# Operands, splits and halos tied to other places of the order in the input projection of a hybrid encoder block

## The chip, the cores and the metric

The kernel runs on one core of a Trainium2 chip. The time is that of one execution on the device, in microseconds (us). A core has a matrix engine (PE, TensorE), three engines for elementwise work (DVE, or VectorE; ACT, or ScalarE; POOL, or GpSimd) and SP (SyncE), which issues this kernel's DMAs. Each engine takes its instructions strictly in its own order, and semaphores tie the engines to each other. The profile records one execution.

## The reference

The input x has 2048 tokens of 1024 values. One projection makes 9232 columns of it, from which two mixers and two merging gates are fed:

```python
h = rms_norm(x, norm_pre_g)
proj = einsum('bsd,de->bse', h, w_in)              # 1024 -> 9232
u_a, z_a, q, k, v, o, z_b, gates, g_a, g_b = split(proj)
pooled = multiscale_pool(u_a)                      # centred windows of 2, 4, 8, 16 tokens, minus the token
y_a = (group_linear(pooled, pool_mix_w) * pool_scale) * silu(z_a)
q, k = silu(depthwise_conv5(concat(q, k)))         # 5 taps along the tokens
hb = mlstm(q, k, v, gates, forward) + mlstm(..., backward)   # 4 heads, chunks of 128
y_b = rms_norm_per_head(hb) * mlstm_norm_g * sigmoid(o) * silu(z_b)
merged = sigmoid(g_a + b0) * (y_a @ w_proj_pool) + sigmoid(g_b + b1) * (y_b @ w_proj_mlstm)
return x + rms_norm(merged @ w_out, norm_post_g)
```

All arithmetic is in float32, and the result has to be close to the reference at that precision.

## The kernel before

**Stages.** `phase1` is the projection, in two halves of 1024 tokens; in the profile the first half lasts to about 800 us and the second to about 1490. Behind it come the mLSTM (to about 1830), the two projections with the merge, and the output projection with norm and residual (about 2180 to the end). Only `phase1` is changed.

**Float32 in parts.** A float32 operand is split into an upper part, rounded to the matmul's own type, and a lower part, the remainder: `split` lets ACT write the upper part (L98) and lets DVE or POOL subtract it (L102). A product of two split operands is three matmuls (upper by upper, upper by lower, lower by upper; L110, L111, L112, and L500 to L502 in the plain form).

**Pairs.** Each half works through 36 pairs of 128 columns, numbered from 0. Pairs 0 and 1 (the first columns of g_a and g_b) are multiplied plainly while the operands of the other form are still being built (`quarters`). From pair 2 on `strassen` needs 7 products for the 8 of a 2 by 2 block form. The tokens' side has the blocks A11, A12, A22 and the sums S1 to S4; the weights' side has B11, B21, B22 and T1 to T4. The products are added up in PSUM banks A, B, C (two buffers each); ACT copies bank A to p1 (L463), and DVE reads bank B into u2 and u3 (L469, L474). `read_banks` lists these reads and the outputs of DVE. Half of a pair's products are issued together with the first products of the next one. For pairs of kind q, k, v and u `collect` puts the four blocks of the result into two tiles named raw (L684 on ACT, L685 on DVE).

**The tokens' operands** are made by `operands` in each half. x comes in as eight tiles that lie in places of other pools (`room`): raw, acc, and two in the ring wc of split weights. `sums` squares and adds them, four matmuls with a column of ones (ssqp, L258) sum over the partitions, and rstd is spread over partitions by four matmuls (rbp, L183). `busy` (L281) is a matmul whose result nobody reads; one stands ahead of the ssqp matmuls and one behind rbp. `combos` then builds S1, S2, S3 and S4 with DVE and splits them: the lower parts of S1 and S3 by POOL, those of S2 and S4 by DVE.

**The weights' operands.** In the first half `load` fetches a pair's columns (wraw, L346), `prep_w` takes differences on DVE (wt, L426) and splits them, and `keep_w` stores T1 to T4 to DRAM (L413). In the second half `again_w` loads the kept ones back (L389) and splits only B11, B21 and B22. Pools: wraw 3 tiles, wc 10, wt 3, and raw 3, acc 4, p 6 for the rest.

**Beside the pairs.** At the start of each half `gates` multiplies the 16 gate columns into a PSUM tile of the tag tr (gps; two buffers) and ACT copies it out (gsb, L671). In the first half `fold` multiplies pool_mix_w into w_in's u columns (fps, L373, in the same tag) ahead of the pairs that need it. In the second half, `masked` (L1017 on) adds a mask to tiles nm, which lie in the pool wt, on POOL (L1023), and `split_ahead` loads a piece of w_proj_pool (x, tile wp), splits it (upper part in a second tile wp) and stores both. Both stand behind the pair's last weight load (`self.read`). For pairs q and k a convolution of five taps follows (`conv`; ACT L713, DVE L718, POOL L723), for u the sums over windows (L775), for v transposes by PE (vtr, L744) into tiles vn with a column of ones. The second half needs a few columns of the first, the halos, which DVE copies into raw (L705, L765) with zeros at the far end (L706, L766); L737 and L738 write the ones and zeros of vn.

**What sets the order.** The functions issue instructions in program order; a scheduler then makes one order for each engine, from priorities (`tc.high_priority`) and a model of the costs. `tc.issue_after(ins)` puts each instruction issued in its block, if it is of the engine of `ins`, behind `ins` in that engine's order. It adds no wait for other engines.

The prep of pair 2 in the first half is tied behind one of the scalings of x, that of pair 3 to nothing:

```python
with tc.issue_after(self.scaled[8].ins) if i == 2 else ExitStack():
    self.prep_w(W, load(i), wc, wt)
```

Of the kernel before, what the change touches and what calls it, by code (L numbers as in the profile page):

```python
# [81 lines left out]
class Kernel:  # L82
# [122 lines left out]

    def combos(self, H, j, a11, a12, a21, a22):

        nc = self.nc
        s1, s3, s2, s4 = a22, a21, a11, a12
        nc.vector.tensor_tensor(s1, a21, a22, op=ALU.add)  # L210
        nc.vector.tensor_tensor(s3, a11, a21, op=ALU.subtract)
        nc.vector.tensor_tensor(s2, s1, a11, op=ALU.subtract)
        self.put(H, "S2", j, s2, "act", "dve")
        self.put(H, "S1", j, s1, "act", "pool")
        self.put(H, "S3", j, s3, "act", "pool")
        return lambda: (
            nc.vector.tensor_tensor(s4, a12, s2, op=ALU.subtract),
            self.put(H, "S4", j, s4, "act", "dve"),
        )

    def operands(self, half, H, hp, wc, pool, psum):
# [4 lines left out]
        room = {}  # L226
        for b, q, where in ((0, 0, "raw"), (0, 2, "acc"), (0, 1, "acc"), (0, 3, "acc"), (1, 0, "raw"), (1, 2, "raw"), (1, 1, wc), (1, 3, wc)):
            if where is wc:
                t = wc.tile([P, 2, BLK], F32, tag="wc", name=self.nm("xT"))
            else:  # L230
                t = pool.tile([P, 2, BLK], F32, tag=where, name=self.nm("xT"))
            room[b, q] = t
# [15 lines left out]
        def sums():  # L248
            acc = None
            for kt in range(KT):  # L250
                sq = pool.tile([P, BLK], F32, tag="p", name=self.nm("sq"))
                nc.scalar.activation(sq, X[kt][0], AF.Square)
                if acc is not None:
                    nc.vector.tensor_tensor(sq, sq, acc, op=ALU.add)
                acc = sq
            ps = psum.tile([P, 4], F32, tag="tr", name=self.nm("ssqp"), bufs=2)
            for i in range(4):
                nc.tensor.matmul(ps[:, i : i + 1], acc[:, i * P : (i + 1) * P], self.one_c, start=True, stop=True)  # L258
            busy(X[7][0][:, :P], X[7][0])
            ssq = pool.tile([P, 4], F32, tag="ssq", name=self.nm("ssq"), bufs=2)  # L260
            ends = self.rstd_of(ssq, ps, 0, 0)
            self.rows_of(0, 0, rb[:, :BLK], psum)
            busy(self.rstd[:, :1].to_broadcast([P, P]), X[7][0])
            return ends
# [34 lines left out]
        for b in range(2):  # L299
# [22 lines left out]
            yield  # L322
        ends = [self.combos(H, j, X[j][0], X[4 + j][0], X[j][1], X[4 + j][1]) for j in range(4)]
        yield
# [118 lines left out]
    def strassen(self, H, W, psum, pool, out, n=BLK, swap=False):  # L443
# [18 lines left out]
        p1 = pool.tile([P, n], F32, tag="p", name=self.nm("p1"))  # L462
        nc.scalar.activation(p1, bank["A"], AF.Copy)  # L463
        if self.edge:
# [46 lines left out]
    def phase1(self):  # L511
        tc, nc, a = self.tc, self.nc, self.a
        with ExitStack() as es:
# [25 lines left out]
            for half in range(2):  # L539
# [53 lines left out]
                for i in range(2, n):  # L593
# [7 lines left out]
                    with tc.high_priority(offset=200):  # L601
                        if half == 0:
                            with tc.issue_after(self.scaled[8].ins) if i == 2 else ExitStack():
                                self.prep_w(W, load(i), wc, wt)
                        else:
                            self.again_w(W, i, wr, wc)
# [7 lines left out]
                    if half == 1 and PRE <= i < PRE + 2 * KT:  # L614
                        with tc.issue_after(self.read.ins):
                            self.split_ahead(*divmod(i - PRE, KT))
                    if half == 0:
# [10 lines left out]
                    if half == 0 and i in FOLDS[1:]:  # L628
                        next(fold)
                    next(this)  # L630
                    rest = this
                    if half == 0 and i + 1 in FOLDS:
# [25 lines left out]
    def gates(self, half, H, W, psum, pool):  # L658
        nc = self.nc
        for b in range(2):  # L660
# [9 lines left out]
            g = pool.tile([32, BLK], F32, tag="p", name=self.nm("gsb"))  # L670
            nc.scalar.activation(g, ps, AF.Copy)  # L671
            t0 = half * HALF + b * BLK
# [3 lines left out]
    def collect(self, H, W, psum, pool, width, off):  # L676
# [4 lines left out]
        def out(i, ps, add):  # L681
            d = t[i % 2][:, off + (i // 2) * BLK : off + (i // 2 + 1) * BLK]
            if add is None:
                return nc.scalar.activation(d, ps, AF.Copy)  # L684
            return nc.vector.tensor_tensor(d, ps, add, op=ALU.add)  # L685

# [3 lines left out]
    def pair_qk(self, half, kind, h, H, W, psum, pool):  # L690
# [3 lines left out]
        for i in range(2):  # L694
# [9 lines left out]
            else:  # L704
                nc.vector.tensor_copy(raw[:, 0:4], self.halo_qk[:, ct, :])  # L705
                nc.vector.memset(raw[:, HALF + 4 : HALF + 6], 0.0)  # L706
                self.conv(pool, kind, h, i, raw, HALF + 2, HALF - 2)
# [24 lines left out]
    def pair_v(self, half, kind, h, H, W, psum, pool):  # L732
        nc = self.nc
        t = yield from self.collect(H, W, psum, pool, HALF, 0)
        for b in range(2):
            hi, lo = (pool.tile([P, 4, DH + 2], F32R, tag="acc", name=self.nm(f"vn{p}")) for p in "hl")
            nc.vector.memset(hi[:, :, DH:].bitcast(F32), 1.0)  # L737
            nc.vector.memset(lo[:, :, DH:].bitcast(F32), 0.0)  # L738
            for c2 in range(2):
# [11 lines left out]
    def pair_u(self, half, kind, g, H, W, psum, pool):  # L751
# [6 lines left out]
        for i in range(2):  # L758
# [5 lines left out]
            else:  # L764
                nc.vector.tensor_copy(raw[:, 0:16], self.halo_u[:, ct, :])  # L765
                nc.vector.memset(raw[:, HALF + 16 : HALF + 24], 0.0)  # L766
            s, span, at = raw, 1, 8 - w // 2
# [235 lines left out]

    def split_ahead(self, e, kt):

        nc = self.nc
        x, hi = (self.wt_pool.tile([P, 512], F32, tag="wt", name=self.nm("wp")) for _ in range(2))
        nc.sync.dma_start(x, self.a["w_proj_pool"][:, kt, e * 512 : (e + 1) * 512])
        self.split(hi.bitcast(F32R), x.bitcast(F32R), x, "act", "dve")
        for p, t in enumerate((hi, x)):  # L1010
# [716 lines left out]
```

## Time and profile before

| | us |
|---|---|
| median of 3 runs | 2350.88 |
| lowest and highest | 2348.56 and 2352.04 |
| profiled execution | 2351.66 |
| its span, first to last instruction | 2349.9 |
| its mean granted PE clock, of full speed | 0.994 |
| PE busy | 2291.2 (98%) |
| DVE, POOL, ACT busy | 1428.9, 1182.4, 884.2 |

Timeline rows give the start, the duration, the engine, line and operation, the tiles (out<-in) and shapes, a count where several are put together, and in brackets how long the engine was idle before and what ended that. Rows of waits read "engine tile line <- what ended it: us in total, times, longest". In the rows of stretches each engine has its busy time and the number of its instructions; then come the granted clock, the share of the DMA engines' time and the bytes moved.

### The profile page before, as it was taken

The numbers are of one execution on the slowest core, as the hardware profiler recorded it, in microseconds if no ns is written. First come the engines' busy times: TensorE is split into PE (matmuls) and PEld (weight loads), VectorE is DVE, ScalarE is ACT, GpSimd is POOL, SyncE is SP. The second block draws the span as 40 slices with busy tenths as digits, with TensorE's granted clock in tenths as the row PEclk, the third lists the DMA queues.
The fourth block names the chain that finished last, engine by engine and source line by source line (L and its number), as shares of the span: only waits on it lengthen the run. The fifth ranks groups of instructions, "written<-read, shape, count | busy, mean of one in ns | idle before, by whom it ended". The sixth has DMA issues, their size and how long they took to land.

```text
span 2349.9 us, 32919 instructions
## 1 busy us (share of the span) xinstructions
PE 2291.2 (98%) x11545; PEld 1938.3 (82%) x11545; DVE 1428.9 (61%) x2383; ACT 884.2 (38%) x1795; POOL 1182.4 (50%) x917
## 2 busy tenths in 40 slices
PE   7999999999999999999989999999999899999998
PEld 5788888888888788888878788799998688999776
DVE  7765656767765565546656665489886322454765
ACT  5434332433334423322322233477676201111432
POOL 4655555666654534456555555355556200234865
PEclk9999999999999999999999999999999999999999
DMA  5567766766675366788888787777676745687753
GB/s 210 188 245 266 261 218 233 258 233 223 225 281 206 111 215 204 227 295 290 288 295 297 263 296 252 271 242 243 225 219 195 244 141 166 228 269 272 264 191 126
DMA packets 229238, 550.80 MB, mean 234 GB/s; under 512 B 23120, under 2 KB 70352, under 8 KB 229072
## 3 DMA queue, kind: packets, MB, share of 16 engines
q1 hardware_dynamic: 229072, 548.69, 68.2%
q8 instruction: 91, 1.49, 0.3%
q14 instruction: 75, 0.61, 0.1%
HBM read 335.22 MB, written 213.39 MB: 233 GB/s over the span
## 4 chain that ended last, share of the span: by engine, by line
PE 81%; DMA 7%; DVE 6%; issue 2%; POOL 2%; ACT 1%; SPq 1%; DVEq 0%; POOLq 0%; ACTq 0%
PE bankB L110 7%; PE bankB L112 7%; PE bankB L111 7%; PE bankA L110 5%; PE bankA L111 5%; PE bankA L112 5%; PE bankC L110 5%; PE bankC L111 5%; PE bankC L112 5%; PE num L1367 4%; PE pb L1040 3%; PE pb L1038 3%; PE pb L1039 3%; PE paps L1038 2%; PE paps L1039 2%; PE paps L1040 2%
## 5 line engine op out<-in xcount | busy, mean ns | idle before, releaser
L102 POOL TENSOR_TENSOR wB<-wraw,wB 128x512 fp32r<-128x512 f32 x224 | 338.0, 1513 | 302.1 <-ACT wB L98 214.5
L98 ACT ACTIVATE wB<-wraw 128x512 fp32r<-128x512 f32 x228 | 141.8, 625 | 271.8 <-PE bankB L112 133.7
L102 POOL TENSOR_TENSOR wT<-wt,wT 128x512 fp32r<-128x512 f32 x102 | 148.9, 1464 | 132.7 <-ACT wT L98 105.9
L718 DVE SCALAR_TENSOR_TENSOR acc<-raw,conv_w,acc 128x1026 f32<-128x1026 f32 (+1 forms) x96 | 152.2, 1597 | 10.5 <-ACT acc L713 9.7
L1040 PE MATMUL pb<-oxs,w_proj_mlstm 128*128 128x256 f32 x512 | 143.9, 281 | 0.0
L1039 PE MATMUL pb<-oxs,w_proj_mlstm 128*128 128x256 f32 x512 | 143.8, 281 | 0.0
L1038 PE MATMUL pb<-oxs,w_proj_mlstm 128*128 128x256 f32 x512 | 143.8, 281 | 0.0
L98 ACT ACTIVATE wT<-wt 128x512 fp32r<-128x512 f32 x136 | 85.2, 629 | 150.1 <-PE bankB L112 57.1
L1351 POOL TENSOR_TENSOR qs<-q,isc 128x256 f32<-128x256 f32 x120 | 89.8, 752 | 85.3 <-PE num L1367 53.9
L110 PE MATMUL bankB<-S3h,wT 128*128 128x512 f32 x272 | 106.7, 392 | 3.7 <-DVE u L469 3.7
L110 PE MATMUL bankB<-A22h,wT 128*128 128x512 f32 x272 | 106.3, 391 | 2.9 <-DVE u L474 2.9
L1038 PE MATMUL paps<-pys,w_proj_pool 128*128 128x512 f32 x256 | 102.0, 399 | 6.2 <-DMA w_proj_pool<-wp 3.8
L110 PE MATMUL bankA<-A12h,wB 128*128 128x512 f32 x272 | 107.9, 397 | 0.0
L110 PE MATMUL bankC<-S4h,wB 128*128 128x512 f32 x272 | 106.2, 391 | 1.2 <-DVE raw L685 1.2
L111 PE MATMUL bankB<-S2l,wT 128*128 128x512 f32 x272 | 106.6, 392 | 0.0
L112 PE MATMUL bankB<-S2h,wT 128*128 128x512 f32 x272 | 106.0, 390 | 0.7 <-DVE wT L102 0.7
L112 PE MATMUL bankB<-S3h,wT 128*128 128x512 f32 x272 | 106.6, 392 | 0.0
L111 PE MATMUL bankB<-S3l,wT 128*128 128x512 f32 x272 | 106.6, 392 | 0.0
L110 PE MATMUL bankC<-S1h,wT 128*128 128x512 f32 x272 | 106.5, 392 | 0.0
L111 PE MATMUL bankC<-S4l,wB 128*128 128x512 f32 x272 | 106.4, 391 | 0.0
L110 PE MATMUL bankA<-A11h,wB 128*128 128x512 f32 x272 | 106.2, 390 | 0.0
L112 PE MATMUL bankA<-A12h,wB 128*128 128x512 f32 x272 | 106.1, 390 | 0.0
(413 smaller groups left out, 7063.6 us busy)
## 6 DMA issues: line engine op xcount, KB each, us to landing
wt<-wT SPq DMA_DIRECT2D x136, 512.0 KB, 4.6
wT<-wt SPq DMA_DIRECT2D x136, 512.0 KB, 5.9
wraw<-in_w_in SPq DMA_DIRECT2D x98, 512.0 KB, 5.2
vh<-vnh SPq DMA_DIRECT2D x16, 516.0 KB, 3.9
vl<-vnl SPq DMA_DIRECT2D x16, 516.0 KB, 5.9
v<-vh SPq DMA_DIRECT2D x16, 516.0 KB, 8.8
v<-vl SPq DMA_DIRECT2D x16, 516.0 KB, 8.2
xT<-in_xT SPq DMA_DIRECT2D x16, 512.0 KB, 6.3
```

What stands on the lines that cost most here:

```text
L98: self.upper = nc.scalar.activation(hi, x, AF.Copy)
L102: return eng.tensor_tensor(lo, x, hi.bitcast(F32), op=ALU.subtract)
L110: nc.tensor.matmul(ps, wh, xh, start=start and kt == 0, stop=False, skip_group_check=True)
L111: nc.tensor.matmul(ps, wh, xl, start=False, stop=False, skip_group_check=True)
L112: end = nc.tensor.matmul(ps, wl, xh, start=False, stop=stop and kt == 3, skip_group_check=True)
L718: nc.vector.scalar_tensor_tensor(acc[:, :n], raw[:, tap : tap + n], self.cw[:, ct, tap : tap + 1], acc[:, :n], op0=ALU.mult, op1=ALU.add,)
L1038: nc.tensor.matmul(ps, wh, xh, start=i == 0, stop=False)
L1039: nc.tensor.matmul(ps, wh, xl, start=False, stop=False)
L1040: nc.tensor.matmul(ps, wl, xh, start=False, stop=i == n)
L1351: nc.gpsimd.tensor_tensor(qs[d], q[:, :, ck], isc[:, d, j % 2, None, :].to_broadcast([P, 2, P]), op=ALU.mult)
L1367: nc.tensor.matmul(pn, qs[d][:, kt, :], state[:, kt, :], start=kt == 0, stop=False)
```

## The change

1. Of the eight x tiles, those of the second 512 tokens change places: quarters 2 and 3 now lie in the ring wc, and quarter 1 in raw (before 1 and 3 in wc, 2 in raw).
2. S1's lower parts are made by DVE in the first half, and by POOL in the second as before.
3. The first `busy` is tied behind the last ssqp matmul, and the second is issued twice.
4. The preparation of pair 3 in the first half is tied, which takes hold of its splits on ACT, behind the last sigmoid of pairs 0 and 1 (`evac`) and behind the copy gsb (`gated`).
5. `split_ahead` becomes two functions. `fetch_ahead` loads the piece at the old place; the split comes after the pair's third part was issued, tied on ACT behind p1 of the pair, and on DVE behind its output block 3.
6. In the second half the halo copies, the zeros beside them, and the ones and zeros of vn are tied on DVE behind the last collecting add (`collected`).

```diff
-    def combos(self, H, j, a11, a12, a21, a22):
+    def combos(self, H, j, a11, a12, a21, a22, le):
...
-        self.put(H, "S1", j, s1, "act", "pool")
+        self.put(H, "S1", j, s1, "act", le)
...
-        for b, q, where in (..., (1, 0, "raw"), (1, 2, "raw"), (1, 1, wc), (1, 3, wc)):
+        for b, q, where in (..., (1, 0, "raw"), (1, 1, "raw"), (1, 2, wc), (1, 3, wc)):
...
-                nc.tensor.matmul(ps[:, i : i + 1], acc[:, i * P : (i + 1) * P], self.one_c, start=True, stop=True)
-            busy(X[7][0][:, :P], X[7][0])
+                done = nc.tensor.matmul(
+                    ps[:, i : i + 1], acc[:, i * P : (i + 1) * P], self.one_c, start=True, stop=True
+                )
+            with tc.issue_after(done.ins):
+                busy(X[7][0][:, :P], X[7][0])
...
-            busy(self.rstd[:, :1].to_broadcast([P, P]), X[7][0])
+            for _ in range(2):
+                busy(self.rstd[:, :1].to_broadcast([P, P]), X[7][0])
...
-        ends = [self.combos(H, j, X[j][0], X[4 + j][0], X[j][1], X[4 + j][1]) for j in range(4)]
+        ends = [self.combos(H, j, X[j][0], X[4 + j][0], X[j][1], X[4 + j][1], ("dve", "pool")[half]) for j in range(4)]
...
-        nc.scalar.activation(p1, bank["A"], AF.Copy)
+        self.first_copy = nc.scalar.activation(p1, bank["A"], AF.Copy)
...
-                            with tc.issue_after(self.scaled[8].ins) if i == 2 else ExitStack():
+                            ties = [self.scaled[8]] if i == 2 else [self.evac, self.gated] if i == 3 else []
+                            with ExitStack() as behind:
+                                for t in ties:
+                                    behind.enter_context(tc.issue_after(t.ins))
                                 self.prep_w(W, load(i), wc, wt)
...
                         with tc.issue_after(self.read.ins):
-                            self.split_ahead(*divmod(i - PRE, KT))
+                            held = self.fetch_ahead(*divmod(i - PRE, KT))
...
                     next(this)
+                    if half == 1 and PRE <= i < PRE + 2 * KT:
+                        self.split_ahead(*held)
...
-            nc.scalar.activation(g, ps, AF.Copy)
+            self.gated = nc.scalar.activation(g, ps, AF.Copy)
...
-            return nc.vector.tensor_tensor(d, ps, add, op=ALU.add)
+            self.collected = nc.vector.tensor_tensor(d, ps, add, op=ALU.add)
+            return self.collected
...
-                nc.vector.tensor_copy(raw[:, 0:4], self.halo_qk[:, ct, :])
-                nc.vector.memset(raw[:, HALF + 4 : HALF + 6], 0.0)
+                with self.tc.issue_after(self.collected.ins):
+                    nc.vector.tensor_copy(raw[:, 0:4], self.halo_qk[:, ct, :])
+                    nc.vector.memset(raw[:, HALF + 4 : HALF + 6], 0.0)
...
-            nc.vector.memset(hi[:, :, DH:].bitcast(F32), 1.0)
-            nc.vector.memset(lo[:, :, DH:].bitcast(F32), 0.0)
+            with self.tc.issue_after(self.collected.ins) if half else ExitStack():
+                nc.vector.memset(hi[:, :, DH:].bitcast(F32), 1.0)
+                nc.vector.memset(lo[:, :, DH:].bitcast(F32), 0.0)
...
-                nc.vector.tensor_copy(raw[:, 0:16], self.halo_u[:, ct, :])
-                nc.vector.memset(raw[:, HALF + 16 : HALF + 24], 0.0)
+                with self.tc.issue_after(self.collected.ins):
+                    nc.vector.tensor_copy(raw[:, 0:16], self.halo_u[:, ct, :])
+                    nc.vector.memset(raw[:, HALF + 16 : HALF + 24], 0.0)
...
-    def split_ahead(self, e, kt):
+    def fetch_ahead(self, e, kt):
...
         nc.sync.dma_start(x, self.a["w_proj_pool"][:, kt, e * 512 : (e + 1) * 512])
-        self.split(hi.bitcast(F32R), x.bitcast(F32R), x, "act", "dve")
+        return e, kt, x, hi
+
+    def split_ahead(self, e, kt, x, hi):
+
+        nc, tc = self.nc, self.tc
+        with tc.issue_after(self.first_copy.ins), tc.issue_after(self.read_banks[-1].ins):
+            self.split(hi.bitcast(F32R), x.bitcast(F32R), x, "act", "dve")
```

The tables that follow show the order of instructions, not their times. On PE, the start of the program, before (numbers in names tell buffers apart):

```order
L281 MATMUL busy_348<-xT_306 128x512
L258 MATMUL ssqp_343<-one_c,sq_340 128x1 x4
L183 MATMUL rbp_353<-ident,rstd 128x128 x4
L281 MATMUL busy_359<-xT_306,rstd 128x512
L500 MATMUL bankA_500<-A11h_402,wB_35_390 128x512
```

and after:

```order
L258 MATMUL ssqp_343<-one_c,sq_340 128x1 x4
L285 MATMUL busy_348<-xT_306 128x512
L183 MATMUL rbp_353<-ident,rstd 128x128 x4
L285 MATMUL busy_359<-xT_306,rstd 128x512
L285 MATMUL busy_361<-xT_306,rstd 128x512
```

The first `busy` stands between ssqp and rbp now, and two follow rbp.

On ACT, in the first half, where the sigmoids (sg) of pairs 0 and 1, the gates' copy (gsb) and the splits of pair 3 (wB and wT from 110 on before, from 111 on after) meet, before:

```order
L98 ACTIVATE wB_95_849<-wraw_821 128x512
L841 ACTIVATE sg_777<-bankC_632,b_merge 128x512
L98 ACTIVATE wB_110_952<-wraw_948 128x512
L841 ACTIVATE sg_780<-bankC_633,b_merge 128x512
L98 ACTIVATE wT_113_959<-wt_957 128x512
L841 ACTIVATE sg_789<-bankA_640,b_merge 128x512
L98 ACTIVATE wT_114_962<-wt_955 128x512
L841 ACTIVATE sg_792<-bankB_641,b_merge 128x512
L671 ACTIVATE gsb_797<-gps_684 32x512
L98 ACTIVATE wT_116_967<-wt_965 128x512
```

and after:

```order
L98 ACTIVATE wB_96_851<-wraw_823 128x512
L854 ACTIVATE sg_779<-bankC_634,b_merge 128x512
L854 ACTIVATE sg_782<-bankC_635,b_merge 128x512
L854 ACTIVATE sg_791<-bankA_642,b_merge 128x512
L854 ACTIVATE sg_794<-bankB_643,b_merge 128x512
L680 ACTIVATE gsb_799<-gps_686 32x512
L98 ACTIVATE wB_111_954<-wraw_950 128x512
L98 ACTIVATE wT_114_961<-wt_959 128x512
```

The splits of pair 3 stood between the sigmoids and ahead of gsb, and all stand behind gsb now. On SP the load of pair 3's second piece (wraw, L346 before and L350 after) stood behind the store of T2, and now stands ahead of all four stores.

On DVE, in the second half, from the pair v of the last head to the pair u behind it (raw_1405 and 1406 are v's tiles before, 1406 and 1407 after; u2 and u3 read the banks of the pair u), before:

```order
L469 TENSOR_TENSOR u2_1433_9714<-bankB_1430_9686,p1_1432_9700 128x512
L737 MEMSET vnh_1439_9788 128x4x2
L765 COPY raw_1428_9684<-halo_u_215 128x16
L766 MEMSET raw_1428_9684 128x8
L685 TENSOR_TENSOR raw_1405_9528<-bankB_1408_9531,p1_1410_9545 128x512
L738 MEMSET vnl_1440_9789 128x4x2
L685 TENSOR_TENSOR raw_1406_9529<-bankC_1409_9532,u2_1411_9559 128x512
L474 TENSOR_TENSOR u3_1434_9766<-bankB_1430_9686,p1_1432_9700 128x512
L685 TENSOR_TENSOR raw_1428_9684<-bankC_1431_9687,u3_1434_9766 128x512
```

and after:

```order
L473 TENSOR_TENSOR u2_1434_9712<-bankB_1431_9684,p1_1433_9698 128x512
L694 TENSOR_TENSOR raw_1406_9526<-bankB_1409_9529,p1_1411_9543 128x512
L694 TENSOR_TENSOR raw_1407_9527<-bankC_1410_9530,u2_1412_9557 128x512
L749 MEMSET vnh_1436_9766 128x4x2
L750 MEMSET vnl_1437_9767 128x4x2
L749 MEMSET vnh_1440_9786 128x4x2
L750 MEMSET vnl_1441_9787 128x4x2
L478 TENSOR_TENSOR u3_1435_9764<-bankB_1431_9684,p1_1433_9698 128x512
L694 TENSOR_TENSOR raw_1429_9682<-bankC_1432_9685,u3_1435_9764 128x512
L102 TENSOR_TENSOR wp_1426_9678<-wp_1426_9678,wp_1427_9679 128x512
```

The two collecting adds of v stood behind a memset and the halo copy of u, and now stand ahead of all of vn's memsets; u's halo comes later.

More of the change, by code (lines that the diff above doesn't have):

```diff
@@ L226, in operands @@
         room = {}
-        for b, q, where in ((0, 0, "raw"), (0, 2, "acc"), (0, 1, "acc"), (0, 3, "acc"), (1, 0, "raw"), (1, 2, "raw"), (1, 1, wc), (1, 3, wc)):
+        for b, q, where in ((0, 0, "raw"), (0, 2, "acc"), (0, 1, "acc"), (0, 3, "acc"), (1, 0, "raw"), (1, 1, "raw"), (1, 2, wc), (1, 3, wc)):
             if where is wc:
```

## The prediction

> **What bounds the kernel now.** I read first the page's busy shares, then the waits of PE by what ended them (total, times, longest), then the stretches in which PE was not full, and last the rows of those stretches. Of the first two a row each is shown here; other waits follow where they are used.
>
> ```profile
> PE 2291.2 (98%) x11545; PEld 1938.3 (82%) x11545; DVE 1428.9 (61%) x2383; ACT 884.2 (38%) x1795; POOL 1182.4 (50%) x917
> ```
>
> ```profile
> PE fps L373 <- ACT gsb L671: 5.1, 1, 5.1
> ```
>
> PE is busy for 2291.2 of 2349.9 us, so an edit earns only what it takes from PE's waits, or from the time after a wait in which PE's clock is low. The second cost is seen in the stretches (time, PE busy, PEld, DVE, ACT, POOL, granted clock, DMA share, GB/s):
>
> ```profile
> 60.00:80.00 20.00, 19.27 (x84) 14.54 (x83) 20.00 (x18) 8.96 (x16) 14.20 (x9) 1.00 0.04 14
> 80.00:100.00 20.00, 14.93 (x56) 11.93 (x56) 10.66 (x16) 9.68 (x19) 10.89 (x7) 0.83 1.02 361
> 1220.00:1240.00 20.00, 15.08 (x68) 12.15 (x67) 9.07 (x16) 4.88 (x8) 10.35 (x9) 0.91 0.91 275
> 1300.00:1340.00 40.00, 37.70 (x160) 30.75 (x159) 28.68 (x32) 10.34 (x16) 19.43 (x15) 0.96 0.71 235
> ```
>
> In the last three the clock is below 1.00, each time around a wait of more than 2 us, and two of them are places that the change touches. The profiled execution took 2351.66 us, 1.76 more than its span, and the median of the three runs is 2350.88; the sum below is made against 2351.66.
>
> **The start (x tiles, warm-up).** Rows of PE from the sums of squares to full speed:
>
> ```profile
> 11.79 1.87 PE L258 MATMUL ssqp<-one_c,sq 128*128 128x1 f32 x8 [0.55 <-DVE sq L254]
> 15.40 2.08 PE L183 MATMUL rbp<-ident,rstd 128*128 128x128 f32 x8 [1.75 <-POOL rstd L161]
> 17.27 1.91 PE L281 MATMUL busy<-xT,rstd 128*128 128x512 f32 x2
> 20.06 0.79 PE L500 MATMUL bankA<-A11h,wB 128*128 128x512 f32 x1 [0.87 <-ACT A11h L98]
> ...
> 23.63 0.63 PE L502 MATMUL bankA<-A11l,wB 128*128 128x512 f32 x1
> 24.06 0.63 PE L502 MATMUL bankB<-A11l,wB 128*128 128x512 f32 x1
> ...
> 25.05 0.39 PE L500 MATMUL bankA<-A11h,wB 128*128 128x512 f32 x1
> 25.28 0.39 PE L501 MATMUL bankA<-A11h,wB 128*128 128x512 f32 x1
> ```
>
> Two matmuls start 0.43 us apart until 24.8, and 0.23 apart from 25.05. From 20.06 to 24.8 that makes 11 matmuls with 0.20 us too much each, 2.2 us, and some 0.4 for the first, 2.6 in all. One warm-up call is the "x2" row: 1.91 us while the clock is low, half of that when it is full. The change takes the first call from ahead of the ssqp matmuls and puts it into the 1.75 us in which PE waits for rstd; there 11.79 + 1.87 + 1.91 = 15.57 against 15.40 costs 0.2 us at most. The second call is doubled. At low speed the pair ends at 17.27 + 3.8 = 21.1, and the first real matmul, held until 20.06 by the split of A11, would be 1.0 us late; at full speed the pair ends by about 20 and costs nothing. So the end is between -2.6 (all real matmuls at full speed) and +1.2 (none, and the calls in the way). PE has now 9 us without a gap from 11.8 on, where before it had gaps of 1.75 and 0.87; that is nearer to the first end, and I take **-1.5**.
>
> The Trainium skill (TensorE: Matmul & The Clock Gate, Part 1 "The HAM clock gate") says that the clock starts at half and doubles after a window of about 3.4 us in which PE was active, with windows that run on freely. By that rule 9 us without a gap hold a whole window that ends by 18.6 at the latest, and this term would be about -2.4. The trace agrees so far as the clock rose 4.6 us after 20.06, and that is within two such windows.
>
> The place of S1's x tiles (two into the ring of split weights instead of others) changes which tile comes free when, and moves no work; the ring holds 10 tiles, and the weights of pair 2 that take them next are split on DVE at 77.82 (row below), late enough: 0.
>
> **S1's lower parts from POOL to DVE.**
>
> ```profile
> 54.01 6.72 POOL L102 TENSOR_TENSOR S1l<-xT,S1h 128x512 fp32r<-128x512 f32 x4 [3.70 <-ACT S1h L98]
> 56.10 6.88 DVE L211 TENSOR_TENSOR xT<-xT,xT 128x512 f32<-128x512 f32 x4
> 77.82 0.68 DVE L102 TENSOR_TENSOR wT<-wt,wT 128x512 fp32r<-128x512 f32 x1
> 78.56 0.50 PE L112 MATMUL bankB<-S2h,wT 128*128 128x512 f32 x1 [0.70 <-DVE wT L102]
> ```
>
> DVE is busy without a break from 60 to 80 (the row 20.00 above), and PE waits 0.70 for its last product of that row, T2's lower part. A subtraction of 128x512 takes DVE 0.68 alone, and 6.88 / 4 = 1.72 while POOL runs one (6.72 / 4 = 1.68). Four more on DVE cost 2.7 alone or 6.9 beside POOL; four fewer on POOL give back 4 x (1.72 - 0.68) = 4.2. T2 comes between 1.5 earlier and 2.7 later. In DVE's order the four new ones follow the sums S1 closely, while POOL begins its S3 parts only when ACT, which splits S1 first, has split S3; so most of them run alone, and I take the earlier end: the wait of 0.70 goes, with the slower first matmul behind it **-1.0** (bounds -1.0 and +2.7).
>
> **Pair 3's splits behind the gates.** The costliest place of all:
>
> ```profile
> 76.73 1.16 ACT L98 ACTIVATE S4h<-xT 128x512 fp32r<-128x512 f32 x2 [2.19 <-DVE xT L217]
> 80.34 0.64 ACT L98 ACTIVATE wT<-wt 128x512 fp32r<-128x512 f32 x1 [2.46 <-DVE wt L426]
> 81.40 0.67 ACT L841 ACTIVATE sg<-bankC,b_merge 128x512 f32<-128x512 f32 x1
> 84.22 0.79 DVE L426 TENSOR_TENSOR wt<-wraw,wt 128x512 f32<-128x512 f32 x1 [2.10 <-DMA wraw<-in_w_in]
> 85.11 0.63 ACT L98 ACTIVATE wT<-wt 128x512 fp32r<-128x512 f32 x1 [1.94 <-DVE wt L426]
> 87.30 0.57 ACT L671 ACTIVATE gsb<-gps 32x512 f32<-32x512 f32 x1
> 87.92 3.78 PE L373 MATMUL fps<-fm,fw 128*128 128x256 f32 x8 [5.07 <-ACT gsb L671]
> 100.38 0.39 PE L110 MATMUL bankA<-A11h,wB 128*128 128x512 f32 x1
> ```
>
> A weight load lands at 84.2, and DVE's difference waits for it; ACT, which takes its instructions in order, waits with pair 3's split at 85.11 and only then makes the last sigmoids and gsb. Until gsb is out, its PSUM buffer ("tr", two of them) is held, and the second group of folding matmuls stands: 5.07 us. The stretch's clock of 0.83 is 0.17 x 20 / 0.5 = 6.8 us at half speed; fps from 87.92 on and the first matmuls behind it fall into it, some 5 us of work of which half, 2.5, is lost. The place costs 5.1 + 2.5 = 7.6. In the new order on ACT the four sigmoids and gsb stand ahead of pair 3's splits, behind S4's splits (done at 77.9) and two of pair 2, T4's and B22's. T4's waits for a difference on DVE (80.34), which now stands ahead of two of S4's lower parts. So ACT has 2 x 0.64 + 4 x 0.67 + 0.57 = 4.5 us to do behind 77.9, and gsb is out at 82.4. PE asked at 87.92 - 5.07 = 82.85 and, with the 1.0 gained before, asks at 81.9. A wait of 0.5 stays, shorter than those of 0.87 and 0.70 above, behind which the clock didn't fall. On SP the load now stands ahead of four stores, so it doesn't come later. What is late next is pair 3's splits. Its first product began at 100.38, and would begin 8 earlier, at 92. B11's split stands next behind gsb, so its upper part is out by 83 and the lower (POOL, 1.7) by 85; T2's follows the load of 84.2, as now. The cover is 7 us, and what goes beyond it would show on PE one for one. 7.6 less 0.5 is **-7.1**; the bounds are -7.6 and, if T4's split stays at 80.34 (gsb at 84.4, a wait of 2.5 and 1 of slow clock), -4.
>
> **Half 2: projection weights in two steps, halos and ones behind the last collected block.** Rows of DVE and PE there:
>
> ```profile
> 1191.21 2.06 DVE L102 TENSOR_TENSOR wp<-wp,wp 128x512 fp32r<-128x512 f32 x1 [7.24 <-ACT wp L98]
> 1226.07 1.22 DVE L765 COPY raw<-halo_u 128x16 f32<-128x16 f32 x1 [1.96 <-POOL acc L723]
> 1229.50 0.68 DVE L685 TENSOR_TENSOR raw<-bankC,u 128x512 f32<-128x512 f32 x1 [1.60 <-issue]
> 1230.23 1.75 PE L744 MATMUL vtr<-ident,raw 128*128 128x128 f32 x7 [3.95 <-DVE raw L685]
> 1328.24 0.52 PE L110 MATMUL bankB<-S3h,wT 128*128 128x512 f32 x1 [2.30 <-DVE u L469]
> ```
>
> ```profile
> PE vtr L744 <- DVE raw L685: 4.7, 2, 4.0
> PE bankB L110 <- DVE u L469: 3.7, 3, 2.3
> PE bankC L110 <- DVE raw L685: 1.2, 1, 1.2
> PE bankB L110 <- DVE u L474: 0.9, 1, 0.9
> ```
>
> The four rows of waits are all that PE has from 830 to 1400, 10.5 us. At 1191 a bank's read (L474) stands behind a split of wp that waits 7.24 for ACT; with the split a pair later and tied behind p1, the 0.9 goes. From 1224 to 1230 the collecting adds stand behind a memset, a halo copy and (in DVE's order) a second memset, each of which waits for a tile of its own: the new order has both adds first. Of 3.95 nearly all goes, and with it some 8 slow matmuls behind it (1.3): -4.5, allowing for 0.7 by which the transposes now stand three matmuls later on PE. The wait of 2.30 at 1328 is behind the sums of u's windows, which nothing takes away; it can move either way, 0. Of the small ones (1.4 for the two other L469, 0.7 for the other vtr) half: -1.0. The sum is **-6.4**. The lower end is all of the 10.5 us and 3 us of slow clock, -13. Upper end: 24 halos start up to 1.2 us later, and the splits of wp hold two of three tiles in the wt pool longer; if a third of the halos' delay reached PE, 24 x 0.4 = 9.6 against the gain, +3.
>
> **Sum:** 2351.66 - 1.5 - 1.0 - 7.1 - 6.4 = 2335.7, say **2336**. The program after 1490 us keeps its order, and gets 0.
>
> **Rivals.**
>
> *Only the first stage gains* (half 2 at 0): 2351.66 - 9.6 = 2342.1. For it: the order of half 2 changes on SP and DVE almost everywhere, and waits for tiles are handed on. Against: two of the four waits have their cause in what is moved.
>
> *The gates' wait stays in another form* (3 us more of it kept, half 2 as forecast): 2339; or with the stage at nothing and half 2 whole, 2351.66 - 2.5 - 6.4 = 2343. For it: from 80 to 100 us the DMA engines are full (share 1.02), so a load issued earlier needn't land earlier; against: gsb no longer stands behind any load.
>
> *Nothing is gained in sum*: the gates' place wins 4 only and the other parts come out at their upper ends, 2351.66 - 4 + 1.2 + 2.7 + 3 = 2354.6, or half way to them, 2350. For it: each part moves work on DVE, which is full from 60 to 80 us and has to read PE's banks in half 2. Against: it takes three mishaps with three causes.
>
> *Slower:* the split of wp holds two of the three wt tiles from the load to the later split, and the mask tiles (nm) go through the one that is left, each with a load, POOL's add and a store. SP issues in order, so the weight loads behind a waiting nm load are late.
>
> ```profile
> POOL nm L1023 <- DMA nm<-negM: 63.5, 20, 6.4
> SPq L1026 <- POOL nm L1023: 23.2, 22, 2.4
> ```
>
> If of 2.4 us, SP's longest hold there, half reached PE in each of the 16 steps, it is +19: 2342.1 + 19 = 2361. It decides from (9.6 + 4.7) / 16 = 0.9 us per step. Against: in the list of half 2 no wait of PE is for a weight, so the loads have some lead now.
>
> **How the numbers follow.** Forecast 0.54, first stage alone 0.18, wait in another form 0.12, nothing 0.07, slower 0.09. A change of 0.2%, 4.7 us, is about what can be told from none: faster is below 2346.2, slower above 2355.6. The first three lie below but for their upper edges (0.03): faster 0.81, same 0.10, slower 0.09. The forecast's own range is 2328 to 2341 (bounds of half 2 and of the warm-up); with the first rivals taken in, 2327 to 2348.
>
> **What would show it.** The wait of fps for gsb gone and clock 1.00 from 80 to 100; full clock before 24 us; no wait of the vtr matmuls near 1230; PE's busy share up by half a per cent. I am wrong if a new wait of over 2 us stands in half 1 behind pair 3's splits, if PE shows waits for wT, wB or DMA in half 2, or if the bank reads (L469, L474) wait behind convolution taps more often than the four times in this list.

## The result, and the profile after

The changed kernel took 2375.9 us (median of 4 runs, 2371.1 to 2377.4), the kernel before 2349.7 (4 runs): a ratio of 1.0107 with a 95% interval of 1.0092 to 1.0121. It is slower by 26 us where 2336 and a gain were forecast. The profiled execution took 2377.38 us.

The page, the waits of PE and its stretches after the change; the last two rows of the third fence hold the places that stood near 1224 and 1328 us in the profile before.

```profile
PE 2296.6 (97%) x11547; PEld 1938.2 (82%) x11547; DVE 1412.7 (59%) x2387; ACT 881.9 (37%) x1795; POOL 1186.5 (50%) x913
```

```profile
PE bankB L110 <- DVE u L478: 20.1, 9, 10.2
PE bankB L110 <- DVE u L473: 14.8, 6, 5.4
...
PE vtr L756 <- DVE vnl L102: 3.1, 1, 3.1
```

```profile
80.00:100.00 20.00, 14.56 (x56) 11.61 (x55) 12.05 (x15) 6.15 (x13) 11.27 (x8) 0.83 0.83 274
...
1100.00:1200.00 100.00, 83.14 (x346) 66.37 (x345) 54.86 (x59) 29.51 (x48) 48.11 (x30) 0.93 0.78 253
1200.00:1300.00 100.00, 96.90 (x428) 79.69 (x427) 57.00 (x73) 28.00 (x46) 54.19 (x37) 0.98 0.82 285
1300.00:1400.00 100.00, 90.19 (x377) 72.38 (x376) 60.85 (x69) 28.88 (x45) 60.53 (x39) 0.97 0.80 273
```

The same stretches before:

```profile
1100.00:1200.00 100.00, 99.12 (x438) 81.75 (x437) 56.98 (x64) 31.32 (x51) 57.44 (x38) 1.00 0.88 297
1200.00:1300.00 100.00, 94.66 (x418) 77.72 (x417) 63.96 (x78) 30.10 (x48) 51.32 (x35) 0.98 0.86 295
1300.00:1400.00 100.00, 97.70 (x424) 80.45 (x423) 64.34 (x68) 29.67 (x45) 59.72 (x41) 0.98 0.81 277
```

PE lost 16 us between 1100 and 1200 and 7.5 between 1300 and 1400, won 2.2 between 1200 and 1300, and the clock fell with the longer waits. Most of it is behind the bank reads u2 and u3 (L473, L478 now), of which no row was over 2.3 us before; one wait of 2.0 us, near 1151, is for a load of kept weights (wT). From 80 to 100 the stretch looks as it did, with 0.83 again, though gsb no longer holds anything. Two places carry most of it.

**The first place, 80 to 100 us.** Rows of ACT, DVE and PE after the change:

```profile
78.81 0.57 ACT L680 ACTIVATE gsb<-gps 32x512 f32<-32x512 f32 x1
83.43 1.67 ACT L98 ACTIVATE wT<-wt 128x512 fp32r<-128x512 f32 x3 [3.54 <-DVE wt L430]
85.01 0.58 ACT L467 ACTIVATE p<-bankA 128x512 f32<-128x512 f32 x1
85.96 1.74 DVE L430 TENSOR_TENSOR wt<-wraw,wt 128x512 f32<-128x512 f32 x1 [1.17 <-POOL wT L102]
87.73 1.64 DVE L430 TENSOR_TENSOR wt<-wraw 128x512 f32<-128x512 f32 x1
89.30 0.68 DVE L473 TENSOR_TENSOR u<-bankB,p 128x512 f32<-128x512 f32 x1
90.03 0.79 PE L110 MATMUL bankB<-S3h,wT 128*128 128x512 f32 x1 [5.44 <-DVE u L473]
```

gsb is out at 79.4 and the folding matmuls run through without a wait. But p1 stands on ACT behind pair 3's splits, and u2 stands on DVE behind differences of pairs 3 and 4, which wait for POOL. PE has come 10 us earlier to the product that overwrites bank B (at 84.6 instead of 94.9), and waits 5.44 us for u2: the wait of 5.07 for gsb came back with another name.

**The second place, the second half.** Waits of SP, POOL and ACT from 800 to 1500 us after the change (the row of POOL read 63.5 before):

```profile
SPq L1045 <- DMA nm<-negM: 58.2, 25, 5.0
SPq L1038 <- DMA wp<-wp: 25.4, 9, 4.3
SPq L1021 <- DMA nm<-nm: 17.6, 9, 3.6
POOL nm L1042 <- DMA nm<-negM: 155.2, 30, 12.1
```

L1038 and L1045 load and store the mask tiles nm, L1021 loads a piece of the projection weights (wp). The load of a mask now waits for a store of wp to land, and the load of wp for the store of a mask, since both live in the three tiles of the pool wt; the store of a mask waits for its own late load (58.2, and 14.0 before). None of the rows of before has SP waiting at a mask load for wp. How one such turn reaches PE, in order of time:

```profile
1160.89 0.32 SPq L1045 DMA_DIRECT2D nm<-nm  x1
1164.93 0.33 SPq L1021 DMA_DIRECT2D wp<-in_w_proj_pool  x1
1167.70 0.63 ACT L98 ACTIVATE wp<-wp 128x512 fp32r<-128x512 f32 x1 [5.62 <-DMA wp<-in_w_proj_pool]
1168.24 1.99 ACT L733 ACTIVATE raw<-acc 128x1026 f32<-128x1026 f32 x2
1169.37 4.76 POOL L734 TENSOR_TENSOR acc<-acc,raw 128x1026 f32<-128x1026 f32 x2 [4.51 <-ACT raw L733]
1174.92 2.38 SPq L735 DMA_DIRECT2D qT<-acc  x2
1183.05 1.24 ACT L724 ACTIVATE acc<-late,conv_b,conv_w 128x1022 f32<-128x1022 f32 x1 [11.26 <-DMA qT<-acc]
1184.33 3.58 DVE L729 SCALAR_TENSOR_TENSOR acc<-late,conv_w,acc 128x1022 f32<-128x1022 f32 x2 [9.64 <-DMA nm<-nm]
1187.83 0.68 DVE L478 TENSOR_TENSOR u<-bankB,p 128x512 f32<-128x512 f32 x1
1188.56 0.80 PE L110 MATMUL bankB<-A22h,wT 128*128 128x512 f32 x1 [10.16 <-DVE u L478]
```

The mask's store, issued at 1160.9, gives up its tile 4 us later; only then does SP issue the next wp load. ACT waits for it with the convolution's sigmoid (L733) behind; POOL's product, the store of qT and with it an acc tile are late; the next convolution starts late on ACT and DVE, and u3 stands behind its taps. PE waits 10.16 us. (DVE's 9.64 is put down to a mask store that ended last, but the convolution's first step on ACT, at 1183, is what its taps read.)

### The profile page after: what moved, and what is told of

Same layout as the page of the kernel before. It is cut to its first block, busy times and chain, and to the rows that moved or that the text cites. A ratio compares the mean times of both kernels' runs of the same rounds, so it can differ in the third digit from the quotient of the medians.

```text
span 2375.6 us, 32930 instructions
## 1 busy us (share of the span) xinstructions
PE 2296.6 (97%) x11547; PEld 1938.2 (82%) x11547; DVE 1412.7 (59%) x2387; ACT 881.9 (37%) x1795; POOL 1186.5 (50%) x913
## 5 line engine op out<-in xcount | busy, mean ns | idle before, releaser
L729 DVE SCALAR_TENSOR_TENSOR acc<-raw,conv_w,acc 128x1026 f32<-128x1026 f32 (+1 forms) x96 | 146.7, 1557 | 21.4 <-ACT acc L724 20.9
L1042 POOL TENSOR_TENSOR nm<-nm,mask 128x256 f32<-128x256 f32 x64 | 67.3, 1064 | 178.3 <-DMA nm<-negM 155.2
L110 PE MATMUL bankB<-A22h,wT 128*128 128x512 f32 x272 | 108.0, 397 | 17.7 <-DVE u L478 17.7
L110 PE MATMUL bankB<-S3h,wT 128*128 128x512 f32 x272 | 108.7, 400 | 12.6 <-DVE u L473 12.6
L473 DVE TENSOR_TENSOR u<-bankB,p 128x512 f32<-128x512 f32 x76 | 52.1, 685 | 103.1 <-PE bankB L112 95.0
L110 PE MATMUL bankB<-S2h,wT 128*128 128x512 f32 x272 | 107.0, 393 | 2.0 <-DMA wT<-wt 2.0
L110 PE MATMUL bankC<-S4h,wB 128*128 128x512 f32 x272 | 106.6, 392 | 1.6 <-DVE u L852 0.9
L430 DVE TENSOR_TENSOR wt<-wraw,wt 128x512 f32<-128x512 f32 x68 | 63.0, 927 | 75.1 <-POOL wT L102 55.8
L110 PE MATMUL bankA<-A12h,wB 128*128 128x512 f32 x272 | 107.6, 395 | 0.0
L112 PE MATMUL bankB<-S2h,wT 128*128 128x512 f32 x272 | 106.9, 393 | 0.0
```

Of the source, the lines that this page charges most:

```text
L110: nc.tensor.matmul(ps, wh, xh, start=start and kt == 0, stop=False, skip_group_check=True)
L112: end = nc.tensor.matmul(ps, wl, xh, start=False, stop=stop and kt == 3, skip_group_check=True)
L430: nc.vector.tensor_tensor(t, x, y, op=ALU.subtract)
L729: nc.vector.scalar_tensor_tensor(acc[:, :n], raw[:, tap : tap + n], self.cw[:, ct, tap : tap + 1], acc[:, :n], op0=ALU.mult, op1=ALU.add,)
L1042: nc.gpsimd.tensor_tensor(t[:, d, :, :], t[:, d, :, :], mask[:, d, None, :].to_broadcast([P, 2, P]), op=ALU.add)
```

## The experiments

Each ratio below is taken against runs of the kernel before that were made beside it. Their medians were 2346.8 to 2347.8 us, so a ratio of 1 means about 2347 and not the 2349.7 of the first four runs.

The theories were, at first: W, the two tiles of wp are held from the load to the late split; H, the halos' ties make convolutions late; S, any tie shakes the scheduler's order.

**Part 5 undone** (the piece is loaded and split in one step at the old place; `split_now` is `split_ahead` as it was before):

```diff
-                            held = self.fetch_ahead(*divmod(i - PRE, KT))
+                            self.split_now(*divmod(i - PRE, KT))
...
-                        self.split_ahead(*held)
```

> The changed kernel with the projection weights' piece loaded and split in one step at the old place again (part 5 undone), all else as changed. Theory W (the piece's two tiles hold two of the three wt tiles from the load to the late split, the mask tiles and SP's order queue behind them): the 24 us of new waits in the second half go, 2344 us (2338 to 2352), and ACT's split of wp no longer waits over 10 us at once. Rival H (the halos behind the collected block make convolutions late): it stays above 2368. Rival S (any tie shakes the scheduler's order, both parts have a share): 2355 to 2366.

2349.8 us, ratio 1.0012 [1.0002, 1.0022]. 26 us are gone: the two-step split makes the loss. That ACT waits less for wp was wrong: its longest wait is still 10.9 us, and 13.9 with a tile of nm, and does no harm there.

**Part 6 undone** (the halos of q, k and u and vn's ones and zeros untied, each as in the lines shown), the two-step split kept:

```diff
-                with self.tc.issue_after(self.collected.ins):
-                    nc.vector.tensor_copy(raw[:, 0:4], self.halo_qk[:, ct, :])
+                nc.vector.tensor_copy(raw[:, 0:4], self.halo_qk[:, ct, :])
...
```

> The changed kernel without the ties of halos and of vn's ones and zeros (part 6 undone), two-step split kept. Theory W: still above 2366, with PE's waits behind u3 and u2 (bank B) in the second half. Rival H: 2344 (2338 to 2352). Rival S: 2355 to 2366.

2379.7 us, 1.0129 [1.0101, 1.0158]: H and S fall.

**Parts 5 and 6 undone**, and **parts 4, 5 and 6 undone** (for part 4 the list of ties for pair 3 is left empty):

```diff
-  [self.evac, self.gated] if i == 3 else []
+  []
```

> Parts 5 and 6 both undone: what is left are x tiles, warm-up, S1 by DVE and pair 3's ties. Theory W and rival H both: about 2346, that is 2349.7 less 1.5 for the warm-up, 1.0 for T2's wait and 1 for the gates' place, where after the change a wait of 5.4 us for u2 stands in the place of the 5.1 for gsb. If the recorded 7.1 us of the gates' place were right, 2340.

> Parts 4, 5 and 6 undone: x tiles, warm-up and S1 by DVE alone. 2347 us by the terms 1.5 and 1.0 (2345 to 2350). Beside the run without parts 5 and 6 it prices the tie of pair 3: 7 us if the recorded term is right, 0 to 2 if the wait only moved to u2.

2346.8 us, 1.0001 [0.9991, 1.0012], and 2346.8 us, 0.9999 [0.9989, 1.0008]. The first half's parts win nothing that can be told, and the gates' tie has the same time with and without. The run without part 5 alone, 2349.8, has part 6 more than the first of these two; the 3 us between them lie within intervals that overlap, so that part 6 wins nothing, and a cost of it isn't shown here.

**What of the two steps costs?** Three runs: the load at the late place too; the upper part's tile taken only at the split; the split without its two ties.

```diff
# fetch_late_too: this stands behind next(this), ahead of the split, not ahead of the pair's work
+                        with tc.issue_after(self.read.ins):
+                            held = self.fetch_ahead(*divmod(i - PRE, KT))
                         self.split_ahead(*held)
# one_tile_held: the tile hi is taken in split_ahead
-        x, hi = (self.wt_pool.tile(...) for _ in range(2))
+        x = self.wt_pool.tile(...)
# split_untied
-        with tc.issue_after(self.first_copy.ins), tc.issue_after(self.read_banks[-1].ins):
-            self.split(...)
+        self.split(...)
```

> The changed kernel with the piece of the projection weights loaded at the late place too, directly ahead of its split; the ties of the split stay. No tile of the wt pool is then held between the pair's weight loads and the split. Theory W (tiles held from the load to the split): most of the loss goes, 2352 us (2345 to 2359). Rival K (the place of the split on ACT and DVE, behind p1 and behind output block 3, is what costs): above 2366, as changed.

> The changed kernel with the tile of the upper part taken only at the split: from load to split one of the three wt tiles is held, not two. Theory W: between the two, 2352 to 2368, with SP's wait for the mask tiles behind wp's stores (25 us as changed) at half or less. Rival K: above 2368, since the split stays where it is.

> The changed kernel with the split in two steps but without its two ties. Theory W: two tiles are still held to a split that is issued a pair's third part later, so 2362 to 2380. Rival K: at or under 2353.

2377.7 us, 1.0125 [1.0108, 1.0142]; 2374.7 us, 1.0128 [1.0104, 1.0151]; 2350.6 us, 1.0007 [0.9998, 1.0017]. W falls as it was put: how long the tiles are held ahead of the split does not matter, and the ties do. K, the place of the split, was the better forecast. With one tile held, SP's wait at the mask loads for stores of wp is 27.8 us (25.4 as changed), where W wanted half. The orders on SP show what the ties do to the tiles. With them, around the second half's pairs 15 and 16 (wp_1267 and wp_1266 are the upper and lower part of one piece, wp_1293 is the next piece's tile):

```
L1038 DMA nm_1292_8757<-negM_206 128x256 x2
L1030 DMA wp_61<-wp_1267_8598 128x512
...
L1045 DMA nm8_182<-nm_1292_8757 128x512
L1021 DMA wp_1293_8763<-in_w_proj_pool 128x512
...
L1030 DMA wp_61<-wp_1266_8597 128x512
```

and without them (wp_1294 and wp_1293 are one piece):

```
L1038 DMA nm_1292_8757<-negM_206 128x256 x2
L1021 DMA wp_1293_8763<-in_w_proj_pool 128x512
...
L1030 DMA wp_61<-wp_1294_8764 128x512
L1045 DMA nm8_182<-nm_1292_8757 128x512
L1030 DMA wp_61<-wp_1293_8763 128x512
```

Tied, a piece's stores straddle the next pair's mask and the next piece's load; so at each step a tile is free only once a store has landed. The new theory, W2: the late split gives the tiles back late, and wp and nm then take turns.

**One tie alone**, ACT's or DVE's, and **the masks elsewhere** (all ties kept, the 32 mask tiles made at pairs 28 to 35, while wp has 12 to 27):

```diff
+        with tc.issue_after(self.first_copy.ins):              # act_tie_only
+        with tc.issue_after(self.read_banks[-1].ins):          # dve_tie_only
-  range(max(0, 8 * (i - 10) // 6), max(0, min(32, 8 * (i - 9) // 6)))
+  range(4 * max(0, i - 28), 4 * max(0, i - 27))                # masks_apart
```

> The changed kernel with the split tied on ACT behind p1 alone, and not on DVE. If the lower part's place on DVE, behind output block 3, is what gives the tiles back late, 2350 us (2345 to 2356); if the upper part's place on ACT does, 2366 or more.

> The changed kernel with the split tied on DVE behind output block 3 alone, and not on ACT. The mirror of the run with ACT's tie alone: 2366 or more if DVE's place is what costs, 2350 (2345 to 2356) if ACT's is. If both runs come out near 2376, each tie alone is enough; if both near 2350, it takes the two.

> The changed kernel, two-step split and its ties as they are, but the 32 mask tiles are made at pairs 28 to 35 of the second half, four a pair, where no piece of the projection weights is in the wt pool (pairs 12 to 27 have them). Theory W2 (what costs is that wp and mask tiles take turns in the three wt tiles, and the late split gives them back late, so that SP waits for stores to land): 2350 us (2343 to 2356). Rival K2 (the late place alone: conv, p1 and bank reads stand behind the split on ACT and DVE): 2366 or more.

2353.3 us, 1.0026 [1.0015, 1.0037], with ACT's tie; 2374.6 us, 1.0117 [1.0103, 1.0131], with DVE's: the lower part behind output block 3 is the part that costs, and ACT's tie has a few us at most. With the masks apart 2357.5 us, 1.0047 [1.0031, 1.0063], less good than W2 had it, though the place of the rest is clear. From 1000 to 1300 PE is busy for all of the 300 us, with both ties; the next wait is

```profile
1349.22 0.80 PE L110 MATMUL bankB<-A22h,wT 128*128 128x512 f32 x1 [6.47 <-DVE u L478]
```

at the pairs that now have four masks each. To tell the crowding from the late split, **weights and masks were set apart without crowding**: pieces at pairs 2 to 17, masks at 18 to 33.

```diff
-PRE = 12
+PRE = 2
...
+  range(2 * max(0, i - 18), min(32, 2 * max(0, i - 17)))
```

> The changed kernel with all its ties, but the projection weights' pieces at pairs 2 to 17 (before 12 to 27) and the mask tiles at pairs 18 to 33, two a pair (before four in three pairs from 10 on), so that the two never share the wt pool, and the masks aren't crowded at the end as in the run with masks at 28 to 35. Theory W2 (the whole loss of the two-step split is the sharing of the wt pool): 2349 us or less (2340 to 2352). If the rest of 10 us that the run with the masks at pairs 28 to 35 left had another cause than the crowding (the late split itself): 2355 or more.

2349.2 us, 1.0006 [0.9996, 1.0016]: with every tie in place the loss is gone. So it takes both, the late lower part and the sharing of the pool; to give wp tiles of its own was not tried. How the sharing reaches PE is told above from the rows of one turn, and waits of the same kind stay in this run, where wp and nm no longer share the pool:

```profile
PE bankB L110 <- DVE u L478: 7.3, 3, 6.4
ACT acc L724 <- DMA qT<-acc: 11.5, 1, 11.5
```

What makes these is open. The sum of SP's waits at the four DMAs of wp and nm from 800 to 1500 us, out of each profile, goes with the times here:

| kernel | SP's waits there, us | median, us |
|---|---|---|
| before | 73.7 | 2349.7 (2346.8 to 2347.8 beside the others) |
| two steps undone; split untied | 76.4; 75.2 | 2349.8; 2350.6 |
| weights early, masks late | 82.2 | 2349.2 |
| ACT's tie alone; masks at 28 to 35 | 101.2; 108.8 | 2353.3; 2357.5 |
| halos untied | 162.1 | 2379.7 |
| changed | 175.8 | 2375.9 |
| load late; one tile held; DVE's tie alone | 175.3; 177.4; 181.0 | 2377.7; 2374.7; 2374.6 |

The sum is a sign and not a price: in the fastest kernel below, with the split in one step, it is 108.7 us.

**The first half's wait for u2.** Pair 3's preparation is tied behind p1 (ACT) and u2 (DVE) of pair 2 as well, with parts 5 and 6 undone:

```diff
-  [self.evac, self.gated] if i == 3 else []
+  [self.evac, self.gated, self.first_copy, self.read_banks[0]] if i == 3 else []
```

> Parts 5 and 6 undone, and pair 3's preparation tied also behind p1 on ACT and u2 on DVE of pair 2. In the first half the wait of 5.4 us for u2 behind pair 3's and 4's differences goes, and with it 2.5 us of low clock: by that 2339 (2335 to 2343), beside 2346.8 of the kernel with the first half's parts alone and 2346.8 before. Rival: pair 3's weights, now split later, are late by as much, and a wait for wB or wT of pair 3 stands near 92 us: 2344 to 2348.

2338.9 us, 0.9961 [0.9947, 0.9974]: 9 us faster than before. Its rows at the place:

```profile
78.70 0.57 ACT L467 ACTIVATE p<-bankA 128x512 f32<-128x512 f32 x1
81.19 0.69 DVE L473 TENSOR_TENSOR u<-bankB,p 128x512 f32<-128x512 f32 x1 [0.65 <-DMA sga<-sg]
```

```profile
80.00:100.00 20.00, 20.00 (x90) 16.59 (x89) 14.48 (x19) 9.23 (x17) 14.49 (x10) 1.00 0.94 314
```

u2 comes 8.1 us earlier than in the changed kernel, PE is full from 80 to 100 and the clock stays at 1.00; pair 3's weights are not missed.

**Towards a faster kernel.** To that version were added part 6 for u and v alone; weights and masks apart; and, in the changed kernel with all its parts, the ties for u2 and the setting apart.

> The faster kernel of the runs so far (parts 5 and 6 undone, pair 3 also behind p1 and u2), now with the ties of part 6 for u's halos and for vn's ones and zeros, but not for q's and k's. If these two make the wait of 3.8 us of the vtr matmuls near 1216 and q's and k's make the new waits of part 6: 2335 us (2331 to 2339). If part 6 costs by them: 2341 or more.

> The faster kernel (parts 5 and 6 undone, pair 3 also behind p1 and u2; 2339) with weights at pairs 2 to 17 and masks at 18 to 33. Theory W2: the one-step split waits for tiles behind masks too (ACT for wp 60 us before), so some of its second half's 10 us of waits go: 2332 to 2338. If those waits have other causes: 2338 to 2341.

> The changed kernel with all of its parts, pair 3 also behind p1 and u2, and weights and masks apart. Theory W2: the parts' own effect without the sharing; the second half gains the 6.4 us that the prediction gave it: 2333 (2328 to 2338). If the late split costs by itself: 2344 or more.

With the halos of u and the ones of vn tied 2346.4 us, 0.9993 [0.9981, 1.0005]: the wait of 3.8 us of the transposes is gone, but waits for u2 (9.5 us in seven, the longest 2.9 at 1137) and u3 (2.4 at 1332) stand in its place. So these ties cost some 7 us, by intervals that don't overlap. From the 1000th matmul of L110 to the start of the last matmul the two profiles differ by 1.3 us only (1489.1 against 1487.8), but the profiled execution of the faster kernel was the slowest of its five; where the 7 us lie is open. With weights and masks apart 2336.4 us, 0.9951 [0.9937, 0.9966], the lowest median of all, though its interval overlaps that of 2338.9; 2338.2, 0.9964 [0.9949, 0.9978], with all parts of the change, where 2333 was expected. The last two overlap, so that the two-step split and the halos, freed of the sharing, give nothing that can be told, and the 6.4 us forecast for the second half did not appear.

**The start in a second execution of the kernel before.**

> The kernel before once more, for a second profile. If the 2.5 us that the profiles give to the warm-up and T2 are there in each execution, pair 2's start and the first slow matmuls come as in the first profile, half speed up to near 24.7; if the clock's windows fall otherwise, full speed comes 3.4 us earlier or later and the gain of the start differs between executions.

2343.2 us, in one execution. Its rows:

```profile
17.14 1.75 PE L281 MATMUL busy<-xT,rstd 128*128 128x512 f32 x2
20.25 0.50 PE L500 MATMUL bankA<-A11h,wB 128*128 128x512 f32 x1 [1.36 <-ACT A11h L98]
20.58 0.39 PE L501 MATMUL bankA<-A11h,wB 128*128 128x512 f32 x1
```

and those of the changed kernel:

```profile
17.28 2.79 PE L285 MATMUL busy<-xT,rstd 128*128 128x512 f32 x4
20.75 0.50 PE L504 MATMUL bankA<-A11h,wB 128*128 128x512 f32 x1 [0.68 <-ACT A11h L98]
21.08 0.39 PE L505 MATMUL bankA<-A11h,wB 128*128 128x512 f32 x1
```

Full speed is there from the first matmuls without the added warm-up too, in spite of 1.36 us of waiting ahead: 4 us sooner than in the first profile.

## Why the prediction was wrong

**The start, -1.5.** Between the two profiles first compared the gain is there to a tenth: the 13th matmul of the plain form starts at 23.60 after the change and at 25.05 before. In the second profile of before it starts at 23.10, without the added calls, and the run with the start's parts alone gives 0.9999. The step that failed is that one execution's slow window stood for the kernel. Of the two answers weighed, the Trainium skill's (TensorE: Matmul & The Clock Gate, Part 1 "The HAM clock gate") names the reason that fits, windows that run on freely. The traces agree: the first full clock is recorded at 24.7 us in the first execution of before and at 18.6 in the second, and in each trace all later changes of the clock lie whole multiples of 3.41 us behind it, so that the grid lies elsewhere in each execution. PE has no gap from 15.27 to 18.89 in the second, and a window that ends at 18.6 fits in there. In the first it has none from 15.40 to 19.18, but the windows end at 17.9, 21.3 and 24.7, and only the last of them is without a gap. In the changed kernel PE has no gap from 11.8 to 20.07, and all 16 profiles with the start's parts run at full speed by 21.1 us. So the calls may help an execution whose windows lie badly; in the medians that can't be told from nothing.

**S1 by DVE, -1.0.** The wait of 0.70 for T2's lower part is gone after the change, as forecast. In the second profile of before there is none for T2, but 1.36 at 74.24 for the lower part of B11, split by POOL. It is too small to be told in the medians.

**The gates' place, -7.1.** That the tie takes gsb out of the way was right: it is out at 79.4, before the forecast's 82.4, and the wait of 0.5 allowed for it didn't come. (That 0.87 and 0.70 of waiting leave the clock up was read from the 0.70 alone; at the 0.87 the clock was still low.) Wrong was the step "what is late next is pair 3's splits", with its cover of 7 us. Pair 3's own products were never late; late was pair 2's bank read u2, which needs p1 behind the splits on ACT and stands behind their differences on DVE. I had asked when the moved weights are needed, and not who stands behind them in the two queues. The place is worth what was said once u2 is ahead too: 2338.9 against 2346.8 with the first half's parts alone, 8 us.

**Half 2, -6.4 with bounds of -13 and +3.** This is where the forecast failed. Parts 5 and 6 came to +26 us where -6.4 stood; of the 40 us between 2335.7 and 2375.9 that is 33, the gates' place has 7 and the first two terms 2.5, and 2 go back because the sum began at 2351.66 and the median of before is 2349.7. Two of its steps are wrong. The split "a pair later" was priced by the bank read that it frees and not by the tiles that it gives back late; the upper bound took a share of the halos' delay only, and nothing for the tiles, which is where the 26 us came from. (The range's upper end, 2341, doesn't follow from its own bounds either: +3 in place of -6.4 gives 2345, and the warm-up's +1.2 with it 2348.) The wait of 3.95 at the transposes did go with the halos' ties, but the run with part 6 and without part 5 is no faster for it.

**The rivals.** The one on the slower side had the right middle, tiles of wt taken in turns and SP held in order, at a chance of 0.09 and 2361. Its price was too low: it took 1.2 us a step, and 26 / 16 = 1.6 a step is what the kernel lost. Its first cause, two tiles held from load to split, was not it: one tile or none held until the split lost the same, and what counts is when the lower part's tile comes free. Its last step, late weight loads, was not it either: from 800 to 1490 PE waited 23.2 us for u2 and u3 and once, 2.0 us, for weights. The rival that the gates' wait stays in another form happened too (0.12). I had put them as alternatives, and both came together.

## What to carry to other kernels

A tie that moves an operation later also moves the moment when its tiles come free: ask which other user takes turns in that pool, and whether the engine that issues its loads works in order. When a wait is taken away, look at the next in-order reader of what PE overwrites next, on each engine on which the moved work now stands ahead of it; here one more tie made 8 us of nothing. And a gain of 2 us read from the start of a single profiled execution should be looked for in a second one first.

## What the runs showed of the hardware

The time until PE runs at full speed differed by 4 us between two executions of the same program, with the same instructions and nearly the same waits ahead (20.58 and 24.8 us). The length of a wait alone doesn't say whether the clock falls: behind 1.98 us (ACT's tie alone, at 1171.0) the granted clock was 0.50 for the next 3.4 us, behind 2.92 us (the halos of u and the ones of vn tied, at 1137.2) it stayed at 1.00. Long waits of ACT for a load were harmless by themselves: with the split untied ACT waited 61.8 us for wp loads and 40.1 for tiles of nm from 800 to 1500, more than the changed kernel's 65.5 for wp loads, at 25 us less in all.
